# Up projection as seven block products, and the MLP in two phases with its inner tiles in DRAM

## The chip, the core and the metric

The kernel runs on one core of a Trainium2 chip. The metric is the device time of one execution in microseconds; the lower the better. Five engines work on it with queues of their own: TensorE (PE: matmuls; PEld: the loads of their stationary operand), VectorE (DVE), ScalarE (ACT), GpSimd (POOL), and SyncE (SP), which here only issues DMAs. A few DMAs are issued by ScalarE and GpSimd.

## The reference

One encoder layer on x of 1024 tokens x 1024 channels, in float32. Token mixing (a Fourier branch and a dilated window attention, merged by gates, then an output projection) is followed by a normalisation; then comes the part that is changed:

```
h  = layer_norm(ALPHA * x + mix)                       # 1024 x 1024
u  = square(relu(h @ w_up + b_up))                     # 1024 x 4096
ff = u @ w_down + b_down                               # 1024 x 1024
out = layer_norm(ALPHA * h + ff)
```

## The kernel before

**Numbers.** Each float32 operand of a matmul is split into a high part (a cast to fp32r, `nc.scalar.copy`) and a remainder (a subtraction), and one product is three matmuls into the same PSUM bank: high x high, high x remainder, remainder x high (`mm3`, lines 75 to 77). `split` (lines 63, 64) makes the two parts, on ScalarE and VectorE.

**Buffers.** All big tiles come from rings with a fixed count of equal slots: `U` (31 slots of 128 x 1024 floats), `wr` (3, raw weights as they arrive), `w` (10, split weights), `S` (8 of half that size, `half`), `PT` (6 of half size, `tmp`). PSUM has 8 banks under four tags: mm 3, s 2, pt 2, o 1. A new tile waits until a slot of its ring has been given back by everything that read it.

**Order.** The program is written as one stream. A planner (the framework's scheduler) places each instruction on its engine's queue: it simulates the engines with costs of its own, and among the instructions that are ready in that simulation and have a slot it takes the one written first. The queues run in the order so fixed; waits on semaphores hold what the plan had wrong. `with tc.issue_after(ins)` keeps the DMAs of a block behind `ins` in their queue. SP's DMAs are in such an order too, so a DMA that waits for a slot holds those behind it.

**The layer up to the MLP** (lines 80 to 699) isn't changed but for its last loop. That loop (from line 666) makes the output projection for two halves `hf` of the tokens, each in two halves `c` of the channels and four tiles `t` of 128 tokens. When both channel halves of a token tile are there, VectorE, ScalarE and GpSimd normalise it (lines 687 to 697): `h` is the normalised tile and `ac` is ALPHA * h + ALPHA * b1 + b_down, the start of the accumulator `acc`. `transposed` (line 651) then turns `h` on TensorE, four 128 x 128 transposes into one bank, and splits the result out of PSUM into `h1h` and `h1l`, channels on the partitions. The last tiles of a half are turned later (`late`), between other matmuls.

**The MLP before** takes the 4096 inner channels as 32 tiles `f` of 128. The up projection of a tile and a token half `c` is `up_piece` (line 800): 8 k-tiles x 3 matmuls of 128 x 512 into one bank, ReLU with bias on ScalarE, the square on VectorE. The down projection of 14 pairs of tiles uses a scheme with seven block products in place of eight: with inner tiles as A (A11, A12, A21, A22: two tiles by two token halves) and down weights as B (two tiles by two channel halves), `hidden_blocks` and `down_blocks` form sums of blocks (S1 to S4, T1 to T4) and split them; `down_steps` multiplies A11 B11, A12 B21, S2 T2, S3 T3, A22 T4, S1 T1, S4 B22. Several products are added up in the same banks as they go, and after each product VectorE adds the bank into `acc` (line 824). The loop over pairs runs the up pieces of the next pair between the products of this one. The last four tiles (28 to 31) are done plainly by `up` and `down`, and `finish` normalises and stores each token tile. `acc` (8 tiles of U) stays in SBUF all the time.

## Time and profile before

| | |
|---|---|
| median of 3 runs | 1681.54 us (1681.03 to 1685.92) |
| the profiled execution | 1682.96 us, of which 1680.9 us is its span from the first to the last instruction |
| TensorE's granted clock, mean | 0.992 |
| output projection ends | about 972.5 us into the span |
| busy in the span | PE 1632.9, PEld 1328.6, DVE 866.3, ACT 552.9, POOL 377.1 us |

In the rows of the profile "L64" is a line of the kernel (helpers have one line for all their callers), "w<-wr,w" says which tile is written from which, "x119" is the count, and what follows the last bar is the engine's idle time just before these instructions, with what ended it. Matmuls overlap one another, so the mean of one matmul (some 400 ns) is not what one costs.

### The profile page before, as it was taken

The page shows a single profiled execution, that of the slowest core. Times are in us where ns is not written, and L with a number is a line of the kernel's source. Part 1 is how long each engine was busy: PE and PEld are TensorE (multiplying, and loading weights), DVE is VectorE, ACT ScalarE, POOL GpSimd, SP SyncE. Part 2 cuts the span into 40 slices and gives each one's busy share as a digit, 9 for nine tenths or more (in the row PEclk, how much of TensorE's full clock was granted, in tenths as well). Part 3 has the DMA queues.
Part 4 walks back from the last instruction along what each step waited for, and adds up shares of the span by engine and source line. Part 5 has one row for each costly group of instructions (what it writes and reads, how often), then busy time and mean ns, then how long its engine had stood idle before and what let it go on. Part 6 is the DMA issues. An engine that isn't in the chain of part 4 may idle for free.

```text
span 1680.9 us, 20802 instructions
## 1 busy us (share of the span) xinstructions
PE 1632.9 (97%) x7948; PEld 1328.6 (79%) x7948; DVE 866.3 (52%) x1663; ACT 552.9 (33%) x1160; POOL 377.1 (22%) x359
## 2 busy tenths in 40 slices
PE   8999999999999989999999988999999999999997
PEld 6779777897777778888887766777777777777785
DVE  4240322212342566654257767666666666666658
ACT  4150433313453542322124243333333333333322
POOL 0000000000000120000003246444444444444204
PEclk9999999999999999999999999999999999999998
DMA  7210211111111243552133201111111111111212
GB/s 219 79 49 20 81 60 45 45 51 54 46 57 68 90 142 115 160 160 82 38 132 115 92 26 41 49 51 50 50 50 50 51 50 51 51 50 51 79 40 94
DMA packets 47069, 121.19 MB, mean 72 GB/s; under 512 B 8648, under 2 KB 12168, under 8 KB 46970
## 3 DMA queue, kind: packets, MB, share of 16 engines
q1 hardware_dynamic: 43866, 113.28, 20.7%
q0 software_dynamic: 1824, 6.39, 1.0%
q8 instruction: 62, 1.02, 0.3%
q10 hardware_dynamic: 1280, 0.20, 0.1%
q14 instruction: 37, 0.30, 0.1%
HBM read 108.97 MB, written 10.88 MB: 71 GB/s over the span
## 4 chain that ended last, share of the span: by engine, by line
PE 86%; DVE 5%; ACT 3%; issue 3%; POOL 2%; DMA 1%; DVEq 0%; SPq 0%; POOLq 0%; ACTq 0%
PE pmm L75 20%; PE pmm L76 19%; PE pmm L77 19%; PE ps L75 4%; PE ps L77 4%; PE ps L76 4%; PE ppt L75 3%; PE ppt L77 3%; PE ppt L76 3%; PE po L291 2%; PE ps L237 2%; ACT prob L248 2%; PE ppt L262 2%; DVE z L871 1%; ACT o L303 1%
## 5 line engine op out<-in xcount | busy, mean ns | idle before, releaser
L64 DVE TENSOR_TENSOR w<-wr,w 128x1024 fp32r<-128x1024 f32 x119 | 148.1, 1247 | 299.1 <-ACT w L63 291.5
L75 PE MATMUL pmm<-xh,w 128*128 128x512 f32 x640 | 253.2, 396 | 0.5 <-ACT gate L344 0.5
L77 PE MATMUL pmm<-xh,w 128*128 128x512 f32 x640 | 253.5, 396 | 0.0
L76 PE MATMUL pmm<-xl,w 128*128 128x512 f32 x640 | 252.7, 395 | 0.0
L63 ACT CAST w<-wr 128x1024 fp32r<-128x1024 f32 x119 | 125.0, 1051 | 322.2 <-PE pmm L76 251.0
L75 PE MATMUL pmm<-h1h,w 128*128 128x512 f32 x512 | 202.7, 397 | 0.0
L76 PE MATMUL pmm<-h1l,w 128*128 128x512 f32 x512 | 202.4, 395 | 0.0
L77 PE MATMUL pmm<-h1h,w 128*128 128x512 f32 x512 | 201.9, 394 | 0.0
L76 PEld LDWEIGHTS pmm<-xl,w 128*128 128x128 f32 x640 | 120.2, 188 | 29.2 <-issue 1.2
L75 PEld LDWEIGHTS pmm<-xh,w 128*128 128x128 f32 x640 | 120.3, 188 | 28.7 <-issue 1.5
L77 PEld LDWEIGHTS pmm<-xh,w 128*128 128x128 f32 x640 | 120.2, 188 | 28.0 <-issue 0.7
L824 DVE TENSOR_TENSOR z<-z,ps 128x512 f32<-128x512 f32 x168 | 114.1, 680 | 33.6 <-PE ps L77 33.6
L755 POOL TENSOR_TENSOR part<-q,part 128x512 fp32r<-128x512 f32 x84 | 114.4, 1388 | 38.0 <-ACT part L745 38.0
L75 PEld LDWEIGHTS pmm<-h1h,w 128*128 128x128 f32 x512 | 96.6, 189 | 23.5 <-ACT h1h L63 0.3
L77 PEld LDWEIGHTS pmm<-h1h,w 128*128 128x128 f32 x512 | 96.5, 188 | 23.0
L824 DVE TENSOR_TENSOR z<-z,ppt 128x512 f32<-128x512 f32 x168 | 114.2, 679 | 0.0
L76 PEld LDWEIGHTS pmm<-h1l,w 128*128 128x128 f32 x512 | 96.7, 189 | 21.9
L806 DVE TENSOR_TENSOR q<-PT 128x512 f32<-128x512 f32 x56 | 46.3, 827 | 129.9 <-ACT PT L805 129.9
L277 POOL MEMSET pt<- 64x128 f32 x80 | 16.0, 200 | 378.2 <-PE po L291 350.4
L248 ACT ACTIVATE prob<-prob,st 128x192 f32<-128x192 f32 (+2 forms) x192 | 83.9, 438 | 30.9 <-DVE st L245 30.5
L745 ACT CAST part<-wr 128x512 fp32r<-128x512 f32 x84 | 50.6, 620 | 116.2 <-PE pmm L76 61.6
L697 POOL TENSOR_TENSOR z<-z,b_down 128x1024 f32<-128x1024 f32 x8 | 20.9, 2616 | 300.3 <-ACT z L691 300.3
(352 smaller groups left out, 3161.9 us busy)
## 6 DMA issues: line engine op xcount, KB each, us to landing
wr<-in_wup_dram SPq DMA_DIRECT2D x32, 512.0 KB
wr<-in_wdn_dram SPq DMA_DIRECT2D x32, 512.0 KB
wr<-in_wqk_dram SPq DMA_DIRECT2D x24, 512.0 KB
wr<-in_wout_dram SPq DMA_DIRECT2D x16, 512.0 KB
od<-o POOLq DMA_DIRECT2D x12, 512.0 KB, 3.0
PT<-od SPq DMA_DIRECT2D x24, 256.0 KB
PT<-ad SPq DMA_DIRECT2D x48, 128.0 KB
wr<-in_wv_dram SPq DMA_DIRECT2D x11, 512.0 KB
```

The costliest lines, as they stand in the source:

```text
L63: nc.scalar.copy(h, src)
L64: nc.vector.tensor_tensor(l, src, h.bitcast(F32), op=ALU.subtract)
L75: nc.tensor.matmul(o, lh, rh, start=first, stop=False, skip_group_check=on)
L76: nc.tensor.matmul(o, lh, rl, start=False, stop=False, skip_group_check=on)
L77: nc.tensor.matmul(o, ll, rh, start=False, stop=last, skip_group_check=on)
L237: nc.tensor.matmul(pp[hh][:, step * i:step * i + n], q[r, 128 * b:128 * b + 128], k[r, k0:k0 + n], start=True, stop=True)
L248: nc.scalar.activation(e, e, AF.Exp, bias=m, scale=-1.0, accum_out=st[:, 1, hh, b:b + 1])
L262: nc.tensor.transpose(p[0:p1 - p0, 128 * slot:128 * slot + 128], probs[u][hh][:, i, c0:c0 + p1 - p0], ident)
L745: nc.scalar.copy(t[:, 0], src)
L755: pool(t[:, 1], src, t[:, 0].bitcast(F32), op=ALU.subtract)
L806: nc.vector.tensor_tensor(q, r, r, op=ALU.mult)
L824: nc.vector.tensor_tensor(z, z, p, op=ALU.add)
```

## The change

**Up projection.** Inner tiles are now taken in 16 pairs, and each pair (256 inner channels x 1024 tokens, over 1024 input channels) is computed by seven block products in place of eight: A is the pair's weights (two tiles by two halves of the input channels), B the turned tokens (two channel halves by two token halves). One product is 4 k-tiles x 3 matmuls into one bank. The token blocks B11, B21, T2, T3, T4, T1, B22 are made once, in two parts of 256 columns (`e`), by `plain_block` and `token_blocks`: 28 tiles of U. `transposed` now only copies the turned rows out of PSUM. The weight blocks are made per pair by `weight_tiles` (loads) and `weight_blocks` (sums on VectorE, splits on ScalarE and VectorE). A pair runs in three steps: `step0` (A11 B11, A12 B21), `step1` (S2 T2, S1 T1, S3 T3), `step2` (S4 B22, A22 T4). Bank x goes through A11 B11, S2 T2, S3 T3, A22 T4 and is copied by ScalarE after each of the first three (`keep`); bank z holds S1 T1, then S4 B22 on top; `joined` adds a copy and a bank on VectorE. The `step0` of the first four pairs (START) needs only the first token half and is run ahead of the rest.

**DRAM.** The accumulator's start goes to DRAM (`accd`) and comes back at the start of the down phase. GpSimd forms the sums of the inner blocks, and the seven blocks of each of the 14 pairs are saved to DRAM unsplit (`qd`): A11, A22 and A12 by DMAs that ScalarE issues, S1 to S4 by GpSimd. The last two pairs' inner tiles are saved plainly (`qp`).

**Down projection.** It starts when all inner tiles are done, in groups of four pairs (the last has two). For each of the seven products the A blocks of the group's pairs are read back two at a time, cast on ScalarE, the remainder on GpSimd; the B blocks are made from the raw down weights, which are loaded two pairs to a tile in pieces of 2 KB. The product of all pairs of the group is added up in the bank before VectorE adds it to `acc`. The last four inner tiles are read back and done plainly, with `finish` as before.

```diff
+    accd = dram.tile([8, 128, 1024], F32, name="accd")
     late = []
+    raw = {}
+    TB = {n: ([], []) for n in ("B11", "B21", "T2", "T3", "T4", "T1", "B22")}
     def transposed(hf, t, h):
         tc_ = slice(128 * t, 128 * t + 128)
...
             for i in range(2):
                 dp = 2 * q + i
                 if t == 0:
...
+                    raw[hf, dp] = U([128, 2, 512], name="h1t")
+                (nc.vector.tensor_copy if i else nc.scalar.copy)(
+                    raw[hf, dp][:, :, tc_], p[:, 256 * i:256 * i + 256].rearrange("p (d n) -> p d n", d=2))
+        if hf == 0 and t == 3:
+            plain_block("B11", 0)
+        if hf == 1 and t == 3:
+            for i in range(2):
+                token_blocks(i, 1)
+    def plain_block(name, d0):
+        for dp in range(d0, d0 + 2):
+            h_, l_ = U([128, 2, 512], F32R, "tb"), U([128, 2, 512], F32R, "tb")
+            split(raw[0, dp], h_, l_)
+            for v, x in zip(TB[name], (h_, l_)):
+                v.append(x)
+    def token_blocks(i, e):
+        cs = slice(256 * e, 256 * e + 256)
+        b11, b21, b12, b22 = (raw[f, d][:, :, cs] for f, d in ((0, i), (0, 2 + i), (1, i), (1, 2 + i)))
+        sub = nc.vector.tensor_tensor
+        def put(name, src, eng=nc.vector):
+            if e == 0:
+                for v in TB[name]:
+                    v.append(U([128, 2, 512], F32R, "tb"))
+            h_, l_ = (v[i][:, :, cs] for v in TB[name])
+            nc.scalar.copy(h_, src)
+            eng.tensor_tensor(l_, src, h_.bitcast(F32), op=ALU.subtract)
+        t3 = tmp([128, 2, 256], name="t3")
+        nc.gpsimd.tensor_tensor(t3, b22, b12, op=ALU.subtract)
+        sub(b12, b12, b11, op=ALU.subtract)
+        sub(b11, b22, b12, op=ALU.subtract)
+        put("T2", b11)
+        put("T3", t3, nc.gpsimd)
+        sub(b21, b21, b11, op=ALU.subtract)
+        put("T4", b21)
+        put("T1", b12)
+        put("B22", b22, nc.gpsimd)
+    def weight_tiles(pair, both=True):
+        r = []
+        for i in range(2 if both else 1):
+            r.append((U if i and START < pair < 15 else wr)([128, 1024], name="wup"))
+            last = nc.sync.dma_start(r[i], a["wup"][2 * pair + i].rearrange("p k c -> p (k c)"))
+        WR[pair] = r, last.ins
+    def weight_blocks(pair, which):
+        (wa, *wb), _ = WR.pop(pair)
+        out = WB[pair]
+        def put(name, src):
+            t = out[name] = wh([128, 2, 512], F32R, "wb")
+            split(src, t[:, 0], t[:, 1])
+        sum_ = nc.vector.tensor_tensor
+        a11, a12 = wa[:, :512], wa[:, 512:]
+        if which != 1:
+            put("A11", a11)
+            put("A12", a12)
+        if which == 0:
+            return
+        a21, a22 = wb[0][:, :512], wb[0][:, 512:]
+        s3 = tmp([128, 512], name="s3")
+        sum_(s3, a11, a21, op=ALU.subtract)
+        sum_(a21, a21, a22, op=ALU.add)
+        sum_(a11, a21, a11, op=ALU.subtract)
+        put("S2", a11)
+        put("S1", a21)
+        put("S3", s3)
+        sum_(a12, a12, a11, op=ALU.subtract)
+        put("S4", a12)
+        put("A22", a22)
+    START = 4
+    WB = [{} for _ in range(16)]
+    WR = {}
...
                     nc.gpsimd.tensor_tensor(ac, ac, bdn, op=ALU.add)
-                    acc.append(ac)
+                    nc.sync.dma_start(accd[4 * hf + t], ac)
                     late.append((hf, t, h))
...
+    def block_steps(pair):
+        w = WB[pair]
+        ba, bb = bup[:, 2 * pair:2 * pair + 1], bup[:, 2 * pair + 1:2 * pair + 2]
+        bank, part = {}, {}
+        def product(x, y, b, tag=None):
+            first = tag is not None
+            if first:
+                bank[b] = ps(tag)
+            for k in range(4):
+                ks = slice(128 * k, 128 * k + 128)
+                h_, l_ = (v[k // 2][:, k % 2] for v in TB[y])
+                mm3(bank[b], w[x][:, 0, ks], w[x][:, 1, ks], h_, l_, first and k == 0, k == 3, True)
+        def keep(name):
+            part[name] = tmp([128, 512], name="part")
+            nc.scalar.copy(part[name], bank["x"])
+        def done(name, src, bias):
+            r, q = tmp([128, 512]), half([128, 512], name="q")
+            nc.scalar.activation(r, src, AF.Relu, bias=bias)
+            nc.vector.tensor_tensor(q, r, r, op=ALU.mult)
+            return q
+        def joined(name, b):
+            t = part[name]
+            nc.vector.tensor_tensor(t, t, bank[b], op=ALU.add)
+            return t
+        pool = nc.gpsimd.tensor_tensor
+        q = {}
+        strassen = pair < PAIRS
+        def save(name, t):
+            if strassen:
+                (nc.gpsimd if name[0] == "S" else nc.scalar).dma_start(qd[pair, NAMES.index(name)], t)
+        def plain(i, c, t):
+            if not strassen:
+                nc.scalar.dma_start(qp[2 * (pair - PAIRS) + i, :, 512 * c:512 * c + 512], t)
+        def step0():
+            product("A11", "B11", "x", "o" if pair == 3 else "mm")
+            keep("r1")
+            product("A12", "B21", "y", "pt")
+            q[11] = done("A11", joined("r1", "y"), ba)
+            save("A11", q[11])
+            plain(0, 0, q[11])
+        def step1():
+            product("S2", "T2", "x")
+            keep("r2")
+            product("S1", "T1", "z", "s")
+            product("S3", "T3", "x")
+            keep("r3")
+            q[22] = done("A22", joined("r3", "z"), bb)
+            save("A22", q[22])
+            plain(1, 1, q[22])
+        def step2():
+            product("S4", "B22", "z")
+            q[21] = done("A21", joined("r2", "z"), ba)
+            plain(0, 1, q[21])
+            if strassen:
+                s3 = half([128, 512], name="q")
+                pool(s3, q[11], q[21], op=ALU.subtract)
+                save("S3", s3)
+                pool(q[21], q[21], q[22], op=ALU.add)
+                save("S1", q[21])
+                pool(q[11], q[21], q[11], op=ALU.subtract)
+                save("S2", q[11])
+            product("A22", "T4", "x")
+            q[12] = done("A12", bank["x"], bb)
+            save("A12", q[12])
+            plain(1, 0, q[12])
+            if strassen:
+                s4 = half([128, 512], name="q")
+                pool(s4, q[12], q[11], op=ALU.subtract)
+                save("S4", s4)
+        return [step0, step1, step2]
+    NAMES = ("A11", "A12", "S2", "S3", "A22", "S1", "S4")
+    PAIRS = 14
+    qd = dram.tile([PAIRS, 7, 128, 512], F32, name="qd")
+    qp = dram.tile([32 - 2 * PAIRS, 128, 1024], F32, name="qp")
+    plain_block("B21", 2)
+    for x in range(START):
+        weight_tiles(x, False)
+        weight_blocks(x, 0)
+    steps = [block_steps(x) for x in range(16)]
+    for x in range(START):
+        steps[x][0]()
+        if x == 0:
+            while late:
+                if late[0][1] == 3:
+                    for i in range(2):
+                        token_blocks(i, 0)
                 transposed(*late.pop(0))
...
+    for x in range(2):
+        weight_tiles(x)
+    weight_blocks(0, 1)
+    for x in range(16):
+        if x < 13:
+            weight_tiles(x + 2)
+        if x < 15:
+            weight_blocks(x + 1, 2 if START <= x + 1 < 15 else 1)
+        if x == 13:
+            weight_tiles(15, False)
+            weight_blocks(15, 0)
+            weight_tiles(15)
+            last = WR[15][1]
+        steps[x][1]()
+        for nxt in {13: (14, 15), 14: ()}.get(x, (x + 1,)):
+            if START <= nxt < 16:
+                steps[nxt][0]()
+        steps[x][2]()
+        WB[x].clear()
+    def b_raw(pair):
+        r = {}
+        for i in range(2):
+            for c in range(2):
+                t = r[i, c] = U([128, 2, 512])
+                nc.sync.dma_start(t, a["wdn"][2 * pair + i:2 * pair + i + 3:2, :, 512 * c:512 * c + 512]
+                                  .rearrange("b p n -> p b n"))
+        return r
+    def b_raws(p0, n):
+        return [b_raw(p0 + d) for d in range(0, n, 2)]
+    def rest_raws():
+        r = []
+        for f in range(2 * PAIRS, 32):
+            r.append(U([128, 1024], name="wdn"))
+            nc.sync.dma_start(r[-1], a["wdn"][f])
+        return r
+    load = [None]
+    with tc.issue_after(last):
+        r0 = b_raws(0, 4)
+    acc = []
+    with tc.issue_after(last):
         for t in range(8):
...
+            acc.append(U([128, 1024], name="acc"))
+            nc.sync.dma_start(acc[t], accd[t])
+    def a_block(name, pair):
+        r = wr([128, 2, 512])
+        load[0] = nc.sync.dma_start(r, qd[pair:pair + 2, NAMES.index(name)].rearrange("b p n -> p b n")).ins
+        h_, l_ = U([128, 2, 512], F32R), U([128, 2, 512], F32R)
+        nc.scalar.copy(h_, r)
+        nc.gpsimd.tensor_tensor(l_, r, h_.bitcast(F32), op=ALU.subtract)
+        return h_, l_
+    def b_split(src):
+        h_, l_ = wh([128, 2, 512], F32R), wh([128, 2, 512], F32R)
+        split(src, h_, l_)
+        return h_, l_
+    ORDER = (("A11", "B11"), ("A12", "B21"), ("S2", "T2"), ("S3", "T3"), ("A22", "T4"), ("S1", "T1"), ("S4", "B22"))
+    def b_block(name, r):
+        b11, b12, b21, b22 = r[0, 0], r[0, 1], r[1, 0], r[1, 1]
+        sub = nc.vector.tensor_tensor
+        if name == "B11":
+            return b_split(b11)
+        if name == "B21":
+            return b_split(b21)
+        if name == "T2":
+            t3 = r["t3"] = U([128, 2, 512])
+            nc.gpsimd.tensor_tensor(t3, b22, b12, op=ALU.subtract)
+            sub(b11, t3, b11, op=ALU.add)
+            return b_split(b11)
+        if name == "T3":
+            return b_split(r["t3"])
+        if name == "T4":
+            sub(b21, b21, b11, op=ALU.subtract)
+            return b_split(b21)
+        if name == "T1":
+            sub(b12, b22, b11, op=ALU.subtract)
+            return b_split(b12)
+        return b_split(b22)
+    def add_up(p0, n, r, then):
+        def blocks(i):
+            x, y = ORDER[i]
+            return [a_block(x, p0 + d) for d in range(0, n, 2)], [b_block(y, v) for v in r]
         bank = {}
...
+        chain, side = ("s", "s", "pt", "pt"), ("mm", "mm", "mm", "o")
+        def product(tags, new, lo, c, A, B):
             for t in range(4):
...
+                if new:
+                    bank[tags, t] = ps(tags[t])
+                p = bank[tags, t]
+                ts = slice(128 * t, 128 * t + 128)
+                for d in range(n // 2):
+                    for e in range(2):
+                        mm3(p, A[d][0][:, e, ts], A[d][1][:, e, ts], B[d][0][:, e], B[d][1][:, e],
+                            new and d == e == 0, d == n // 2 - 1 and e == 1, True)
                 z = acc[t + lo][:, 512 * c:512 * c + 512]
                 nc.vector.tensor_tensor(z, z, p, op=ALU.add)
...
+        todo = ((chain, True, 0, 0), (side, True, 0, 0), (chain, False, 0, 1), (chain, False, 4, 1),
+                (chain, False, 4, 0), (side, True, 4, 1), (side, False, 0, 1))
+        nxt = blocks(0)
+        for i, how in enumerate(todo):
+            cur = nxt
+            if i < 6:
+                nxt = blocks(i + 1)
+            if i == 4:
+                with tc.issue_after(load[0]):
+                    out = then()
+            product(*how, *cur)
+        return out
+    GROUPS = ((0, 4), (4, 4), (8, 4), (12, 2))
+    for i, (p0, n) in enumerate(GROUPS):
+        r0 = add_up(p0, n, r0, (lambda: b_raws(*GROUPS[i + 1])) if i < 3 else rest_raws)
     g2, b2 = row("ln2_g"), row("ln2_b")
...
+    rest = []
+    for f in range(2 * PAIRS, 32):
+        x, y = wr([128, 1024]), r0[f - 2 * PAIRS]
+        nc.sync.dma_start(x, qp[f - 2 * PAIRS])
+        v = [U([128, 1024], F32R) for _ in range(2)] + [wh([128, 1024], F32R) for _ in range(2)]
+        nc.scalar.copy(v[0], x)
+        nc.gpsimd.tensor_tensor(v[1], x, v[0].bitcast(F32), op=ALU.subtract)
+        split(y, v[2], v[3])
+        rest.append(v)
+    for t in range(8):
+        for c in range(2):
+            s = slice(512 * c, 512 * c + 512)
+            ts = slice(128 * t, 128 * t + 128)
+            p = ps(("s", "pt")[c])
+            for i, (xh_, xl_, yh_, yl_) in enumerate(rest):
+                mm3(p, xh_[:, ts], xl_[:, ts], yh_[:, s], yl_[:, s], i == 0, i == len(rest) - 1)
+            nc.vector.tensor_tensor(acc[t][:, s], acc[t][:, s], p, op=ALU.add)
+        finish(t)
```

More of the change, by code (lines that the diff above doesn't have):

```diff
@@ L697, in tile_hybrid_layer @@
                     nc.gpsimd.tensor_tensor(ac, ac, bdn, op=ALU.add)
-                    acc.append(ac)
+                    nc.sync.dma_start(accd[4 * hf + t], ac)
                     late.append((hf, t, h))
-    hid = {}
-    def up(fs):
-        w = {f: wup[f] if f in wup else weights(a["wup"][f], [128, 8, 128]) for f in fs}
-        for f in fs:
-            hid[f] = U([128, 1024], F32R, "hid"), []
-        for c in range(2):
-            while c and late:
-                transposed(*late.pop(0))
-            for f in fs:
-                p = ps("mm")
-                for k in range(8):
-                    mm3(p, w[f][0][:, k], w[f][1][:, k], h1h[c, k // 2][:, k % 2], h1l[c, k // 2][:, k % 2],
-                        k == 0, k == 7)
-                r, q = tmp([128, 512]), tmp([128, 512])
-                nc.scalar.activation(r, p, AF.Relu, bias=bup[:, f:f + 1])
-                nc.vector.tensor_tensor(q, r, r, op=ALU.mult)
-                l = half([128, 512], F32R, "hidl")
-                split(q, hid[f][0][:, 512 * c:512 * c + 512], l)
-                hid[f][1].append(l)
@@ L722, in down @@
-    def down(fs, after):
-        w = [weights(a["wdn"][f], [128, 1024]) for f in fs]
-        for t in range(8):
-            for c in range(2):
-                s = slice(512 * c, 512 * c + 512)
-                p = ps(("s", "pt")[c])
-                for i, f in enumerate(fs):
-                    hh, ls = hid[f]
-                    mm3(p, hh[:, 128 * t:128 * t + 128], ls[t // 4][:, 128 * (t % 4):128 * (t % 4) + 128],
-                        w[i][0][:, s], w[i][1][:, s], i == 0, i == len(fs) - 1)
-                nc.vector.tensor_tensor(acc[t][:, s], acc[t][:, s], p, op=ALU.add)
-            after(t)
@@ L741, in tile_hybrid_layer @@
-    PAIRS = 14
-    def parts(src, make):
-        t = make([128, 2, 512], F32R, "part")
-        nc.scalar.copy(t[:, 0], src)
-        return t
-    def hidden_blocks(out, q, j):
-        pool = nc.gpsimd.tensor_tensor
-        def put(name, src):
-            t = out[name] = parts(src, U)
-            pool(t[:, 1], src, t[:, 0].bitcast(F32), op=ALU.subtract)
-        if j == 0:
-            put("A11", q[0])
-        elif j == 1:
-            s3 = tmp([128, 512], name="cmb")
-            pool(s3, q[0], q[1], op=ALU.subtract)
-            put("S3", s3)
-        elif j == 2:
-            put("A12", q[2])
-        else:
-            pool(q[1], q[1], q[3], op=ALU.add)
-            pool(q[0], q[1], q[0], op=ALU.subtract)
-            put("S2", q[0])
-            put("A22", q[3])
-            pool(q[2], q[2], q[0], op=ALU.subtract)
-            put("S1", q[1])
-            put("S4", q[2])
@@ L800, in up_piece @@
-    def up_piece(w, f, c):
-        p = ps("mm")
-        for k in range(8):
-            mm3(p, w[0][:, k], w[1][:, k], h1h[c, k // 2][:, k % 2], h1l[c, k // 2][:, k % 2], k == 0, k == 7)
-        r, q = tmp([128, 512]), half([128, 512], name="q")
-        nc.scalar.activation(r, p, AF.Relu, bias=bup[:, f:f + 1])
-        nc.vector.tensor_tensor(q, r, r, op=ALU.mult)
-        return q
-    def up_weights(f):
-        return wup[f] if f in wup else weights(a["wup"][f], [128, 8, 128])
-    def down_steps(A, B):
+    def block_steps(pair):
[68 more added lines that the diff above has]
+        return [step0, step1, step2]
@@ L823, in product @@
                 z = acc[t + lo][:, 512 * c:512 * c + 512]
                 nc.vector.tensor_tensor(z, z, p, op=ALU.add)
-        def alone(x, y, c, lo):
-            held = dict(bank)
-            product(x, y, True, c, lo, ("mm",))
-            bank.update(held)
-        return [lambda: (product("A11", "B11", True, 0, 0), alone("A12", "B21", 0, 0)),
-                lambda: (product("S2", "T2", False, 1, 0), product("S3", "T3", False, 1, 4)),
-                lambda: (product("A22", "T4", False, 0, 4), product("S1", "T1", True, 1, 4)),
-                lambda: product("S4", "B22", False, 1, 0)]
@@ L877, in finish @@
             nc.sync.dma_start(out[128 * t:128 * t + 128, s], z[:, s])
-    down(range(2 * PAIRS, 32), finish)
+    rest = []
[16 more added lines that the diff above has]
+        finish(t)
 def onehot():
```

67 lines of the change are left out of this document (removed).

## The prediction

> **What bounds the kernel now.** I read the page first, then the busy time by stretches of the span, then the chain that ended last, and only then the groups of instructions. The page says that TensorE is busy for nearly the whole span:
>
> ```profile
> span 1680.9 us, 20802 instructions
> PE 1632.9 (97%) x7948; PEld 1328.6 (79%) x7948; DVE 866.3 (52%) x1663; ACT 552.9 (33%) x1160; POOL 377.1 (22%) x359
> ```
>
> Ends of matmuls are modelled, so the share alone proves little. I cut the span at the points where the chain of waits leaves TensorE and comes back to it: the end of the output projection (972.5 us), the steady state of the MLP (1020.1), and the point from which VectorE's last normalisations set the pace (1641.6). Columns: stretch, length, then busy time and (count) of PE, PEld, DVE, ACT, POOL, then clock, DMA share, GB/s.
>
> ```profile
> 972.50:1020.10 47.60, 37.29 (x163) 29.36 (x162) 31.39 (x47) 18.86 (x37) 26.18 (x15) 0.96 0.10 31
> 1020.10:1641.60 621.50, 621.02 (x2647) 496.71 (x2648) 391.82 (x608) 183.23 (x287) 262.97 (x201) 1.00 0.15 52
> 1641.60:1681.00 39.40, 27.80 (x120) 22.17 (x118) 34.85 (x72) 9.55 (x18) 18.01 (x12) 0.89 0.25 94
> ```
>
> The middle stretch has 0.5 us without a matmul in 621.5 us, with VectorE at 63% and all the others lower. The MLP is bound by the number of its matmuls, apart from its two ends. The chain that ended last shows the price of one: the same matmul comes back once per pair of hidden tiles,
>
> ```profile
> 1064.75 0.44 PE pmm L75
> ...
> 1106.89 0.43 PE pmm L75
> ...
> 1149.02 0.44 PE pmm L75
> ```
>
> and between two of these lie 96 matmuls of the up projection (4 pieces x 8 x 3) and 84 of the down projection (7 products x 4 x 3). (1149.02 - 1064.75) / 360 = 0.2341 us each.
>
> **The change, part by part.** *Matmuls removed.* Up: 32 x 2 x 8 x 3 = 1536 before; 16 pairs x 7 products x 4 k-tiles x 3 = 1344 after. Down: 14 x 84 + 192 = 1368 before and after, and the 64 transposes stay. So 192 fewer, all from a stretch in which nothing else sets the pace: 192 x 0.2341 = **-44.9 us**. This count is fixed by the code. What follows is what can eat it.
>
> *What the other engines get in steady state.* Prices, from the groups of instructions (busy, mean ns of one):
>
> ```profile
> L64 DVE TENSOR_TENSOR mgl<-mg,mgh 128x512 fp32r<-128x512 f32 x16 | 10.5, 686 | 5.5 <-PE pmm L76 3.5 <-ACT mgh L63 2.1
> L591 DVE TENSOR_TENSOR mg<-mg,gate 128x512 f32<-128x512 f32 x16 | 11.0, 690 | 0.4
> L824 DVE TENSOR_TENSOR z<-z,ps 128x512 f32<-128x512 f32 x168 | 114.1, 680 | 33.6 <-PE ps L77 33.6
> L806 DVE TENSOR_TENSOR q<-PT 128x512 f32<-128x512 f32 x56 | 46.3, 827 | 129.9 <-ACT PT L805 129.9
> L64 DVE TENSOR_TENSOR w<-wr,w 128x1024 fp32r<-128x1024 f32 x119 | 148.1, 1247 | 299.1 <-ACT w L63 291.5 <-PE pmm L76 7.5
> L63 ACT CAST w<-wr 128x1024 fp32r<-128x1024 f32 x119 | 125.0, 1051 | 322.2 <-PE pmm L76 251.0 <-PE ppt L77 24.8 <-DMA wr<-in_wqk_dram 9.2
> L745 ACT CAST part<-wr 128x512 fp32r<-128x512 f32 x84 | 50.6, 620 | 116.2 <-PE pmm L76 61.6 <-PE pmm L77 32.1 <-PE ppt L77 18.2
> L805 ACT ACTIVATE PT<-pmm,bup 128x512 f32<-128x512 f32 x56 | 38.4, 685 | 112.7 <-PE pmm L77 112.7
> L203 ACT COPY qk<-pmm 128x512 f32<-128x512 f32 x24 | 14.0, 584 | 45.5 <-PE pmm L77 45.5
> L755 POOL TENSOR_TENSOR part<-q,part 128x512 fp32r<-128x512 f32 x84 | 114.4, 1388 | 38.0 <-ACT part L745 38.0
> L479 POOL TENSOR_TENSOR sin<-wr,sin 128x1024 fp32r<-128x1024 f32 x2 | 4.9, 2448 | 4.0 <-ACT sin L478 4.0
> L64 DVE TENSOR_TENSOR h1l<-ps,h1h 128x256 fp32r<-128x256 f32 x32 | 13.0, 418 | 3.7 <-ACT h1h L63 3.2
> ```
>
> Saving and loading, from the answers on single tiles, and the GB/s row in 40 slices of the span:
>
> ```profile
> L322 ACTq DMA_DIRECT2D sd<-ss x16: 270/317/566, 100.1 to 249.2; - x16
> L313 POOL DMA_DIRECT2D od<-o x12: 531/531/691, 100.8 to 567.1; - x12
> L806 DVE TENSOR_TENSOR q<-PT x56: 682/692/2173, 985.7 to 1559.7; 128x512 f32<-128x512 f32 x56
> od<-o POOLq DMA_DIRECT2D x12, 512.0 KB, 3.0
> GB/s 219 79 49 20 81 60 45 45 51 54 46 57 68 90 142 115 160 160 82 38 132 115 92 26 41 49 51 50 50 50 50 51 50 51 51 50 51 79 40 94
> ```
>
> A pair of the up phase is 84 x 0.2341 = 19.7 us of TensorE. VectorE: 7 splits and 4 sums at 0.69, 4 squares at 0.83, 3 joins with a bank at 0.68 = 12.9 us. ScalarE: 7 casts at 0.62, 3 copies out of PSUM at 0.58, 4 ReLUs at 0.69, 3 saves at 0.32 = 9.8. GpSimd: 4 sums at 1.39, 4 saves at 0.53 = 7.7. A group of four pairs in the down phase is 336 x 0.2341 = 78.7 us of TensorE against 14 splits and 6 sums at 1.25 and 28 adds at 0.68 = 44 on VectorE, 28 casts at 1.05 = 29 on ScalarE, 14 + 2 passes at 2.45 = 39 on GpSimd. The adds into the accumulator fall from 392 to 112, which pays for VectorE's new work; none of it was on the path, so it earns nothing. DMA: a pair moves 1.05 MB in and 1.84 MB out (147 GB/s), a group 11.5 MB (146 GB/s), three times the MLP's 50 of now, under the 160 to 219 of other slices. All stays hidden as long as no single wait outlasts its cover. Between S2's product and S3's, into the same bank, ScalarE's copy of the bank has one product of cover (2.8 us); between S3 and S4 lie two products of the next pair, except for pairs 0 to 2 and 14, 15, where the next pair's S2 can step in. Bounds for stalls here: none, and 18 us (12 pairs x 1.5, see the second rival); I take 2, since the loop of now, which is as full (VectorE 63%, 12.9 / 19.7 = 65% after), loses 0.5 us in all.
>
> *The start.* The transposes of the normalised rows in this stretch, from the answer on their line and one row of the timeline:
>
> ```profile
> L657 PE MATMUL ps<-ident,h x24: 270/273/476, 972.6 to 994.8; 128*128 128x128 f32 x24
> 994.02 1.06 PE L657 MATMUL ps<-ident,h 128*128 128x128 f32 x8 [2.42 <-DVE h1l L64]
> ```
>
> Before, from 972.5 to 1020.1, TensorE had 163 - 24 transposes = 139 matmuls (32.5 us) and 24 x 0.13 = 3.2 us of transposes: 11.9 us lost. After, it has 96 matmuls on the first token half (step0 of pairs 0 to 3), the 24 transposes, and S2 of pair 0: 25.7 + 2.8 = 28.5 us, to 1001.0. Then it needs T1 of the tokens, which needs the last transposed rows.
>
> ```profile
> 970.00:980.00 10.00, 7.11 (x29) 5.43 (x28) 9.69 (x17) 6.32 (x13) 3.76 (x3) 0.83 0.34 104
> 980.00:990.00 10.00, 10.00 (x50) 8.16 (x48) 7.86 (x13) 4.03 (x8) 7.27 (x4) 1.00 0.01 3
> ```
> ```profile
> 988.11 1.37 DVE L696 SCALAR_TENSOR_TENSOR h<-h,lnq,ln_b 128x1024 f32<-128x1024 f32 x1 [1.48 <-ACT z L691]
> ```
> ```profile
> 994.68 1.67 ACT L63 CAST h1h<-ps 128x256 fp32r<-128x256 f32 x4 [1.33 <-PE ps L657]
> ```
>
> Busy time in two slices of it, the last of the last rows, and four copies out of the transposes' banks, are shown above. From below: the rows are done at 989.5, plus 1.1 for transposes, 1.7 for copies, 12 VectorE operations at 0.69 = 8.3: T1 at 1000.6, nothing lost, **-11.9**. In between: VectorE's own queue. Of its 17.6 us in 970 to 990 about 8.6 are splits that go (8 h1l, two w, three part, one square), 9.0 of normalisation stay; 6 copies at 0.42, 6 weight splits at 0.69, B21's two at 1.25, four joins and squares (5.5), 24 token operations at 0.69 (16.6), 3 sums and 2 splits of pair 0's weights (3.4) make 43.6 us: T1 at 1016.1, 15.1 lost, **+3**. From above, GpSimd's 12 token operations (3 in each of 4 calls) are held against VectorE's. At 1010 to 1020, where GpSimd never rests, both slow down:
>
> ```profile
> 1012.03 1.76 POOL L794 TENSOR_TENSOR wr<-wr,wr 128x512 f32<-128x512 f32 x1
> 1013.75 1.72 POOL L755 TENSOR_TENSOR part<-q,part 128x512 fp32r<-128x512 f32 x1
> 1015.43 1.72 POOL L767 TENSOR_TENSOR q<-q,q 128x512 f32<-128x512 f32 x1
> ```
> ```profile
> 1012.56 1.78 DVE L784 TENSOR_TENSOR part<-cmb,part 128x512 fp32r<-128x512 f32 x1
> 1014.47 4.91 DVE L784 TENSOR_TENSOR part<-wr,part 128x512 fp32r<-128x512 f32 x3
> ```
>
> One operation of each takes about 1.7 us, a VectorE operation 1.0 more than its 0.69: 12 x 1.0 more, T1 at 1028, 27 lost, **+15**. I take +3: the lower bound forgets a queue that was 88% full for these 20 us already.
>
> The Trainium skill (SBUF — State Buffer, section "Who interferes with whom") says that a VectorE instruction with two SBUF inputs contends with a GpSimd instruction that reads SBUF, and that the one issued first blocks the other for its whole length. The trace agrees nearly: 1.72 us for the couple, where 0.69 and 1.3 added give 2.0. By the page's full sum an up pair would need 15 x 0.69 + 7.7 = 18 of its 19.7 us, so the steady part would still be hidden, and the start and the end would be the first rival below.
>
> *The boundary of the phases.* The tokens' 28 U tiles leave 3 of 31. B11's and B21's 8 come free after step0 of pair 15, 144 matmuls (33.7 us) before the up phase ends, enough for the 8 loads of down weights; T2's, T1's and T3's go next, to the accumulator's loads and to the first A11, which needs 1.05 + 2.45 us of cast and remainder while S4 and A22 still run (5.6 us). Nothing lost is the lower bound; the upper is a load (3.0), a cast and two GpSimd passes in a row, 3.0 + 1.05 + 4.9 = 9. I take **+2**. Behind a wait of SP here stand only loads that are needed later.
>
> *The end.* The last group has two pairs, 168 matmuls, 39.3 us, and beside it the last four tiles are read back and split: GpSimd 8 + 4 passes at 2.45 = 29.4, VectorE 7 + 3 + 4 operations at 1.25 = 17.5 plus adds that read PSUM. Hidden if they overlap, 47 - 39 = 8 late if they exclude each other. I take **+2**. The normalisations behind it are unchanged.
>
> Sum: -44.9 + 3 + 2 + 2 + 2 = -35.9 on the profiled execution's 1682.96 us: 1647. The median shown, 1681.54, is 1.4 lower, so **1646** for the median.
>
> **Rivals.** (1) *VectorE and GpSimd exclude each other where TensorE has no cover*, at the start (+15) and before the last four tiles (+8): -44.9 + 15 + 8 + 2 + 2 = 1665. For it: the 1.7 us couples. Against: only 12 GpSimd operations meet the start. (2) *A wait per pair in ScalarE's order.* The ring w has 10 tiles and a pair takes 7, so the next pair's last cast waits until S1's product gives its tile back; if the copy of the bank is queued behind it, S3 waits for 0.62 + 0.58 and hand-overs, 1.5 us, in 12 pairs: 18, so 1663. Against: the planner orders by readiness, and the same kind of ring holds now without loss. (3) *Slower than before*, the same queue carried on: ScalarE also issues saves, and a save waits for VectorE's square. Cast behind S1 (2.81 + 0.62), a square held by GpSimd (2.17, the longest in the row), the issue (0.32) and the copy (0.58) are 6.5 us against 2.8 of cover: 3.7 us in 14 pairs, 52, so 1682.96 - 44.9 + 52 + 7 = 1697. It decides from 2.5 us of standstill in every pair on. Against: the longest square is one of 56, the median is 0.69. (4) *The start gains*: T1 is there in time, -11.9, with 6 for the rest: 1632. (5) *(1) and (2) together*: -1.5, no change.
>
> **How the numbers follow.** Forecast (1638 to 1656) 0.48; (1) 0.17; (2) 0.11; (3) 0.08; (4) 0.12; (5) 0.04. Less than 0.3% (5 us) can't be told from no change here. Faster: 0.48 + 0.17 + 0.11 + 0.12 = 0.88; same 0.04; slower 0.08. The range takes in (1), (2) and most of (4): 1630 to 1674.
>
> **What would show it.** TensorE's count is 7756. In the up phase a pair's period is 19.7 us (rival 2: 21 or more, with gaps between S1 and S3 released by ScalarE; rival 3: 23). Between the output projection's last matmul and S1 of pair 0 some 15 us are lost, ended by VectorE (rival 4: under 5; rival 1: 25, with VectorE's token splits at 1.7 us). A group of the down phase takes 78.7 us. At the boundary there is one gap of a few us, ended by GpSimd or a load. The forecast is wrong if gaps stand inside the groups, ended by a DMA: then the traffic of 146 GB/s, which I take as hidden, is what I misjudged.

## The result, and the profile after

The changed kernel takes 1740.9 us (median, 1739.7 to 1748.7), the kernel before beside it 1681.6: a ratio of 1.0358 (95% interval 1.0328 to 1.0387), slower. The forecast was 1646. The execution that was profiled took 1748.72 us, 65.8 more than that of before. The page after:

```profile
span 1746.9 us, 20677 instructions
PE 1625.9 (93%) x7756; PEld 1319.0 (76%) x7756; DVE 971.6 (56%) x1551; ACT 607.0 (35%) x1194; POOL 398.5 (23%) x333
```

The 192 matmuls are gone (7948 to 7756), but TensorE's busy time fell by 7.0 us only, and the time in which it stands rose from 48 to 121 us. Busy time by stretches of the changed kernel (columns as in the prediction: stretch, length, busy and count of PE, PEld, DVE, ACT, POOL, clock, DMA share, GB/s). They are the start, pairs 0 to 3, pairs 4 to 13, pairs 14 and 15, the boundary with the first group of the down phase, and the rest of that phase:

```profile
972.50:1040.00 67.50, 42.74 (x164) 33.34 (x165) 57.30 (x82) 32.57 (x56) 32.73 (x18) 0.78 0.27 92
1040.00:1110.00 70.00, 63.36 (x240) 48.36 (x239) 52.06 (x56) 25.24 (x43) 23.47 (x24) 0.89 0.36 134
1110.00:1350.00 240.00, 203.86 (x796) 160.89 (x794) 159.04 (x172) 79.81 (x133) 77.62 (x79) 0.91 0.30 112
1350.00:1400.00 50.00, 45.12 (x178) 35.47 (x179) 28.04 (x34) 19.59 (x30) 8.54 (x10) 0.93 0.76 263
1400.00:1450.00 50.00, 42.14 (x176) 33.12 (x175) 39.66 (x29) 19.92 (x22) 39.23 (x14) 0.97 0.50 149
1450.00:1690.00 240.00, 240.00 (x1027) 193.88 (x1027) 181.52 (x159) 82.50 (x83) 132.10 (x46) 0.99 0.44 141
```

The down phase is what was forecast: 240.00 of 240 us busy, with 141 GB/s beside it. The up phase is not: in 240 us VectorE is busy for 66% and the DMA engines for 30%, nothing is full, and yet TensorE stands for 36 us and its clock is 0.91. I took the start of every matmul in the trace and added up what lies beyond 0.234 us between two starts: as idle time where the distance is over 0.5 us, as half clock where it is 0.33 to 0.5.

| stretch | idle | half clock | both | expected in the prediction |
|---|---|---|---|---|
| start, to 1040 (before, to 1020.1: 11.2 + 1.0) | 26.2 | 5.9 | +19.9 against before | +3 |
| pairs 0 to 3 | 9.1 | 5.3 | 14.4 | |
| pairs 4 to 13 | 42.6 | 15.4 | 58.1 | |
| pairs 14 and 15 | 4.2 | 1.2 | 5.4 | all pairs together +2 |
| boundary, first group | 8.7 | 0.8 | 9.5 | +2 |
| 1450 to 1690 | 0.0 | 1.7 | 1.7 | +2 (end) |

With the -44.9 of the matmuls that is +64.1; the kernel before loses 6.0 behind 1020.1 by the same measure, so +58.1 are left. The MLP of the two profiled executions, from the start of the output projection's last matmul to the end of the span, takes 708.7 us before and 767.8 after: 59.1 more, as the medians have it (59.3). The other 6.9 of the 65.8 lie ahead of the MLP, behind 5019 matmuls in both kernels. This is where that last matmul starts, first before, then after:

```profile
972.14 0.40 PE L77 MATMUL pmm<-w,mgl 128*128 128x512 f32 x1
979.07 0.40 PE L77 MATMUL pmm<-w,mgl 128*128 128x512 f32 x1
```

In the twelve traces of this case it starts anywhere from 966.5 to 979.1, so these 6.9 us are no more than what this part varies by. Seven tenths of the loss in the MLP lie in the pairs. TensorE's waits (what it waited for: us in total, times, longest):

```profile
PE pmm L75 <- ACT part L795: 40.0, 13, 5.9
PE ps L658 <- POOL h L765: 13.9, 4, 7.3
PE ppt L75 <- DVE part L805: 13.1, 1, 13.1
PE pmm L75 <- ACT wb L63: 6.1, 3, 4.0
PE ps L75 <- DVE acc L987: 5.7, 1, 5.7
```

The first row is the copy of bank x behind S2's product (`keep("r2")`, line 795): S3 goes into the same bank. One such pause in the timeline (start, length, engine, instruction; in brackets the idle time ahead of it and what ended it):

```profile
1191.61 1.67 POOL L844 TENSOR_TENSOR q<-q,q 128x512 f32<-128x512 f32 x1 [16.91 <-DVE q L800]
...
1192.91 0.91 DVE L800 TENSOR_TENSOR q<-PT 128x512 f32<-128x512 f32 x1 [0.80 <-issue]
...
1193.57 0.56 POOL L814 DMA_DIRECT2D qd<-q  x1 [0.30 <-POOL q L844]
...
1193.74 2.27 DVE L728 TENSOR_TENSOR wup<-wup 128x512 f32<-128x512 f32 x1
...
1194.15 1.30 POOL L846 TENSOR_TENSOR q<-q,q 128x512 f32<-128x512 f32 x1
...
1196.05 2.14 DVE L729 TENSOR_TENSOR wup<-wup,wup 128x512 f32<-128x512 f32 x1
...
1196.33 1.30 POOL L848 TENSOR_TENSOR q<-q,q 128x512 f32<-128x512 f32 x1
...
1198.23 1.14 ACT L63 CAST wb<-wup 128x512 fp32r<-128x512 f32 x2 [5.40 <-DVE wup L729]
1198.23 2.12 DVE L733 TENSOR_TENSOR wup<-wup 128x512 f32<-128x512 f32 x1
...
1199.27 0.61 ACT L63 CAST wb<-s 128x512 fp32r<-128x512 f32 x1
...
1200.44 0.62 ACT L63 CAST wb<-wup 128x512 fp32r<-128x512 f32 x1 [0.56 <-DVE wup L733]
1200.97 0.58 ACT L795 COPY part<-pmm 128x512 f32<-128x512 f32 x1
...
1201.60 0.80 PE L75 MATMUL pmm<-tb,wb 128*128 128x512 f32 x1 [3.75 <-ACT part L795]
...
1202.19 0.63 PE L76 MATMUL pmm<-tb,wb 128*128 128x512 f32 x1
```

Read from the end: TensorE waits for ScalarE's copy. The copy's source, S2's product, was done at about 1194.8, 6 us earlier; but in ScalarE's queue the copy stands behind four casts of the *next* pair's weight sums (S2', S1', S3', S4'), which TensorE needs only a period later. These wait for VectorE's sums, and the sums take 2.1 to 2.3 us in place of 0.69, because GpSimd forms the inner sums (lines 844 to 856) in the same microseconds. After the pause the matmuls come 0.43 us apart. From 1110 to 1360 there are eight pauses of 3.9 us (4.15 from start to start, as the expectations below have it), one of 6.1 and one of 2.0; a period is 25 us where 19.7 were forecast.

### The profile page after: what moved, and what is told of

The parts are those of the page before. It is cut to its first block, busy times and chain, and to the rows that moved or that the text cites. A ratio compares the mean times of both kernels' runs of the same rounds, so it can differ in the third digit from the quotient of the medians.

```text
span 1746.9 us, 20677 instructions
## 1 busy us (share of the span) xinstructions
PE 1625.9 (93%) x7756; PEld 1319.0 (76%) x7756; DVE 971.6 (56%) x1551; ACT 607.0 (35%) x1194; POOL 398.5 (23%) x333
## 5 line engine op out<-in xcount | busy, mean ns | idle before, releaser
L64 DVE TENSOR_TENSOR w<-wr,w 128x1024 fp32r<-128x1024 f32 x83 | 103.5, 1249 | 293.4 <-ACT w L63 293.4
L63 ACT CAST w<-wr 128x1024 fp32r<-128x1024 f32 x83 | 87.1, 1051 | 234.7 <-PE pmm L76 190.7
L933 POOL TENSOR_TENSOR U<-wr,U 128x1024 fp32r<-128x1024 f32 x49 | 143.3, 2944 | 110.3 <-ACT U L932 48.9
L75 PE MATMUL pmm<-tb,wb 128*128 128x512 f32 x240 | 107.4, 448 | 46.1 <-ACT part L795 40.0
L64 DVE TENSOR_TENSOR w<-U,w 128x1024 fp32r<-128x1024 f32 x49 | 103.3, 2110 | 21.9 <-ACT w L63 18.9
L77 PE MATMUL pmm<-tb,wb 128*128 128x512 f32 x240 | 103.3, 431 | 2.8 <-DVE wb L64 2.8
L76 PE MATMUL pmm<-tb,wb 128*128 128x512 f32 x240 | 103.7, 432 | 0.0
L75 PEld LDWEIGHTS pmm<-tb,wb 128*128 128x128 f32 x240 | 50.9, 212 | 64.6 <-ACT part L795 45.7
L63 ACT CAST w<-U 128x1024 fp32r<-128x1024 f32 x49 | 51.3, 1048 | 126.0 <-PE ppt L76 56.0
L768 POOL TENSOR_TENSOR z<-z,b_down 128x1024 f32<-128x1024 f32 x8 | 19.5, 2440 | 309.3 <-ACT z L762 284.0
L63 ACT CAST wb<-wup 128x512 fp32r<-128x512 f32 x96 | 56.6, 618 | 90.2 <-DVE wup L729 75.0
L245 DVE CUSTOM_DVE_ANT_0 prob<-ps,bias 128x192 f32<-128x192 f32 (+2 forms) x192 | 55.8, 347 | 44.6 <-PE ps L237 37.6
L844 POOL TENSOR_TENSOR q<-q,q 128x512 f32<-128x512 f32 x14 | 23.3, 1665 | 226.7 <-DVE q L800 226.7
```

The lines of the kernel that those rows point to most:

```text
L63: nc.scalar.copy(h, src)
L64: nc.vector.tensor_tensor(l, src, h.bitcast(F32), op=ALU.subtract)
L75: nc.tensor.matmul(o, lh, rh, start=first, stop=False, skip_group_check=on)
L76: nc.tensor.matmul(o, lh, rl, start=False, stop=False, skip_group_check=on)
L77: nc.tensor.matmul(o, ll, rh, start=False, stop=last, skip_group_check=on)
L245: nc.vector.tensor_tensor_reduce(out=e, in0=pp[hh][:, step * i:step * i + n], in1=bias[:, hh, bs], scale=-1.0, scalar=3e38, op0=ALU.add, o ...
```

## The experiments

**Theory A:** GpSimd's inner sums hold VectorE's weight sums, and ScalarE's queue carries that delay to a copy that TensorE waits for. **Rivals:** VectorE has simply too much to do (B); the traffic to and from DRAM (C); for the start, couples (D) against the mere length of VectorE's queue (E). A has two links, so the first three runs cut one, the other, and both. "Before" in the same comparisons was 1682.2 to 1684.6 us.

**The queue's order alone.** `weight_blocks` makes the sums where it did and gives back the five casts, which are written behind the pair's step1 (each with its remainder, so VectorE's order moves a little too):

```diff
-            weight_blocks(x + 1, 2 if START <= x + 1 < 15 else 1)
+            casts = weight_blocks(x + 1, 2 if START <= x + 1 < 15 else 1)
...
         steps[x][1]()
+        if x < 15:
+            with tc.issue_after(mark["r2"]):       # behind the copy, on ScalarE
+                casts()
```

> Only ScalarE's order in the up phase is changed: the copy of S2's bank (keep r2) stands ahead of the casts of the next pair's weight sums; VectorE's sums and GpSimd's inner sums stay where they are, so their couples at 2.2 us stay. Theory A (GpSimd slows VectorE's weight sums, and ScalarE's queue carries the delay to the copy that S3 waits for): the 4.15 us gap per pair goes, and with it the half clock behind it; the up phase loses some 58 us less, at most 5 come back at the join of r3 behind the remainders: 1741 - 53 = 1688, period 20 us. Rival B (VectorE has too much to do, whatever the order): the gap moves to S4, which waits for the join, period 23 or more, 1720 to 1741. Rival C (the DRAM traffic of the up phase): no change, 1741.

Measured 1684.35 us, ratio to before 1.0004 (0.9988 to 1.0019). The couples are all still there, the pauses are not. The row of line 728 among the instructions on this tile (times, shortest/median/longest in ns, from when to when), and the stretch of the steady pairs, both of this run:

```profile
L728 DVE TENSOR_TENSOR wup<-wup x16: 691/2268/2276, 1027.0 to 1313.9; 128x512 f32<-128x512 f32 x16
1110.00:1350.00 240.00, 233.31 (x983) 184.27 (x983) 194.68 (x204) 101.36 (x165) 95.94 (x92) 0.99 0.48 173
```

VectorE is busier (81%), the traffic greater (173 GB/s), and TensorE loses some 0.6 us a pair from 1120 to 1300, where a pair takes 20.1 us. That is A's number, and B and C fall: a fuller VectorE and more traffic per microsecond go with less loss.

**The couples alone.** The inner sums on VectorE, ScalarE's order held:

```diff
-        pool = nc.gpsimd.tensor_tensor
+        pool = nc.vector.tensor_tensor
...
+            with tc.issue_after(mark[pair + 1]):   # behind the cast of S4'
+                nc.scalar.copy(part["r2"], bank["x"])
```

> GpSimd's four inner sums per pair are made on VectorE instead; ScalarE's order is held as it was, the copy of S2's bank behind the four casts. Theory A: VectorE's sums fall from 2.2 to 0.69 us; from the square of A12 to the end of the copy it is 5 sums (3.5), a cast and the copy (1.2), 4.7 us where it was 8.2; S3 could start 3.9 us after the square, so a gap of about 0.9 us per pair is left: 58 - 14 x 0.9 = 45 less, 1696. A rival that has the queue's order alone as its cause (contention without effect): the gap stays near 4, 1741. Rival B (too much work on VectorE, which gets 2.8 us more per pair): gaps of over 4, 1741 to 1770.

Measured 1674.35 us, 0.9937 (0.9915 to 0.9960). Line 728's counterpart and the same stretch of this run:

```profile
L730 DVE TENSOR_TENSOR wup<-wup x16: 682/684/692, 1023.7 to 1305.9; 128x512 f32<-128x512 f32 x16
1110.00:1350.00 240.00, 238.93 (x1028) 191.75 (x1027) 168.70 (x246) 101.20 (x166) 45.87 (x49) 1.00 0.51 179
```

The sums are at 0.68 us and the copy, still behind the casts, is in time; the 0.9 us a pair that I had left over for it don't show (a steady pair takes 19.6). So the order alone doesn't lose the time either: it takes both links.

**Both.** The first line of that diff alone; with it the planner itself puts the copy ahead of the casts.

> GpSimd's four inner sums per pair on VectorE, and ScalarE's order left to the planner, which now has the copy of S2's bank ahead of the next pair's casts: both suspected causes are gone. Theory A: no gap above 0.5 us in a pair, period 19.7 us, 1741 - 56 = 1685; the start loses its 23 us still. Rival B (VectorE is full: 15.7 of 19.7 us per pair): period over 21, above 1705. Rival C (traffic): 1741.

Measured 1664.59 us, 0.9883 (0.9862 to 0.9904), faster than before. From 1040 on:

```profile
1040.00:1110.00 70.00, 70.00 (x303) 56.30 (x302) 53.86 (x87) 30.41 (x53) 8.67 (x16) 1.00 0.48 176
1110.00:1350.00 240.00, 238.39 (x1026) 192.26 (x1025) 171.54 (x241) 103.08 (x161) 50.74 (x51) 1.00 0.49 175
```

Every pair takes 19.5 us. It is 20 us better than expected, since I had kept the loss of pairs 0 to 3, 14 and 15 (14.4 + 5.4) as it was, and it went with the same edit.

For the rest, this table goes by the count of matmuls, from the eight transposes ahead of the output projection's last 24 matmuls: the first 204 (32 transposes, those 24, and 148 of the up phase; some 44 us of work), then the mean of 13 times 84 (a pair), and, from 72 matmuls further on, 336 that reach over the boundary into the first group (78 where nothing stalls). The last column is the MLP of the profiled execution, from the projection's last matmul to the end of the span; before it was 708.7. What varies ahead of the MLP from execution to execution is not in these four columns, but it is in the median.

| run | median | ratio to before (95%) | first 204 | a pair | first group | MLP |
|---|---|---|---|---|---|---|
| the change | 1740.9 | 1.036 (1.033 to 1.039) | 77.0 | 25.1 | 89.4 | 767.8 |
| queue's order alone | 1684.4 | 1.000 (0.999 to 1.002) | 75.8 | 20.9 | 87.6 | 709.1 |
| couples alone | 1674.4 | 0.994 (0.992 to 0.996) | 77.2 | 20.4 | 86.8 | 698.2 |
| both | 1664.6 | 0.988 (0.986 to 0.990) | 75.4 | 19.5 | 88.6 | 687.0 |
| tokens on VectorE, nothing else | 1738.4 | 1.031 (1.029 to 1.033) | 71.9 | 25.4 | 87.7 | 764.3 |
| both, new order of the start | 1659.3 | 0.986 (0.982 to 0.989) | 71.7 | 19.5 | 88.4 | 683.1 |
| new order, tokens on VectorE | 1654.8 | 0.981 (0.978 to 0.984) | 69.2 | 19.5 | 88.6 | 681.0 |
| new order, copy first | 1656.0 | 0.984 (0.982 to 0.986) | 66.9 | 19.7 | 87.9 | 680.5 |
| new order, copy first, tokens on VectorE | 1650.8 | 0.981 (0.979 to 0.983) | 62.9 | 19.7 | 88.6 | 677.2 |
| the last, and one more row tile on VectorE | 1650.8 | 0.981 (0.979 to 0.983) | 61.9 | 19.7 | 88.8 | 676.5 |
| new order, copy first, tokens and T3 of the down weights on VectorE | 1649.6 | 0.978 (0.976 to 0.981) | 63.2 | 19.7 | 84.8 | 673.5 |

**The start: couples.** In the changed kernel, `token_blocks` with no GpSimd operation (three of its instructions moved to VectorE).

> The start alone: the 12 token operations of GpSimd (T3 and the remainders of T3 and B22) are made by VectorE, 36 in place of 24 there. Theory D (each engine holds the other, 1.7 us a couple): 24 at about 1.7 us become 36 at 0.69, 41 to 25 us, and the gaps of TensorE between 972 and 1040 us fall by 10 to 16: 1741 - 13 = 1728. Rival E (only the length of VectorE's queue ahead of the joins counts, which is 12 longer): no gain, 1741 to 1750. The up phase behind it stays as it was.

Measured 1738.44 us. TensorE's waits in this run:

```profile
PE ppt L75 <- DVE part L805: 7.5, 1, 7.5
PE pmm L75 <- ACT wb L63: 8.7, 3, 6.6
```

The pause for the joins (line 805) fell from 13.1 to 7.5, with 12 more operations in VectorE's queue, so the couples have a part in it (D); but the next one, for pair 0's weight casts, grew from 4.0 to 6.6. The first 204 matmuls gained 5.1 us and the total 2.5, not 13. Something else in that queue is behind it.

**The start: the order on VectorE.** On top of "both", the queue in the order in which TensorE needs it (shortened; `token_blocks_2` takes T4 and B22 over from `token_blocks`):

```diff
         put("T2", b11)
+        put("T1", b12)
         put("T3", t3, nc.gpsimd)
-        sub(b21, b21, b11, op=ALU.subtract)
-        put("T4", b21)
-        put("T1", b12)
-        put("B22", b22, nc.gpsimd)
...
+        if x == 1:                               # behind step0 of pairs 0 and 1
+            for e in range(2):
+                for i in range(2):
+                    token_blocks(i, e)
+            for y in range(2):
+                weight_tiles(y)
+            weight_blocks(0, 1)
...
+    for e in range(2):                           # behind step0 of pairs 2 and 3
+        for i in range(2):
+            token_blocks_2(i, e)                 # T4 and B22
```

> On top of the inner sums on VectorE (1664.6), only the order of the start: VectorE gets the joins of pairs 0 and 1, then the token operations of T2, T1 and T3, then pair 0's weight sums, then the joins of pairs 2 and 3, and T4 and B22 last. Theory D (S2 of pair 0 comes late because VectorE's queue holds the joins, T4 and B22 ahead of its weight sums): from the join of pair 1 (996) 16 token operations with couples (18 us), four sums and one remainder (4.2): S2 at 1018 instead of 1028.6, so 10 less, 1655. Rival F (something outside VectorE's order sets the start: the last transposed rows, the loads of the weights): gain under 3, 1662 to 1667.

> The same order, and besides no GpSimd work on tokens (T3 and the remainders of T3 and B22 on VectorE) and all copies out of the transposes' banks on ScalarE: no couples in the start. Theory D with couples: 24 token operations at 0.61 (14.6) and 4.2 behind the join of pair 1, S2 at 1015, the copies 2 more: 13 to 15 less than 1664.6, 1650. If the couples cost as much as the operations they replace, it is level with the run before it. Rival F: no gain, 1662 to 1667.

Measured 1659.32 and 1654.83 us. In the first, S2 of pair 0 starts 38.9 us behind the output projection's last matmul in place of 54.9, 15.9 us earlier; of that, 3.7 are left at the end of the first 204 matmuls. TensorE's waits in its start say where the rest went:

```profile
PE ps L658 <- POOL h L769: 7.3, 1, 7.3
PE pmm L75 <- ACT part L799: 5.6, 1, 5.6
PE pmm L75 <- ACT wb L63: 2.9, 1, 2.9
PE ps L75 <- DVE part L809: 2.6, 1, 2.6
```

The second row is the old acquaintance: the copy of S2's bank, now behind the casts of T4 and B22, whose sources VectorE hadn't made. I had written them there myself. So the next run moves them behind step1:

```diff
         steps[x][1]()
+        if x == 0:
+            for e in range(2):
+                for i in range(2):
+                    token_blocks_2(i, e)
```

> The run with the new order of the start (1659.3), and only T4's and B22's token operations are written behind pair 0's step1, so that ScalarE's copy of S2's bank stands ahead of all but one of their casts. Theory (the same cause as in the up phase: a copy that TensorE waits for stands behind casts whose source is late): the gap of 6.0 us in front of S3 of pair 0 falls below 1, and with the half clock behind it 5 to 7 us go: 1653. Rival G (VectorE, which has no pause from 1000 to 1037 there, sets the pace, so the gap only moves to S4): 1657 to 1661.

> The same step on the run without GpSimd work on tokens (1654.8), whose gap in front of S3 is 3.5 us: by the theory 3 to 4 us less, 1651; by rival G no change, 1653 to 1656.

Measured 1655.95 and 1650.84 us, 3.4 and 4.0 less. The waits in the start of the first:

```profile
PE ps L658 <- POOL h L769: 7.8, 2, 7.3
PE pmm L75 <- ACT wb L63: 7.1, 2, 3.8
PE pmm L75 <- ACT part L799: 1.7, 2, 1.0
```

The copy's wait is gone (5.6 to 1.0 at most). The intervals of these runs overlap with those above them, so for single steps of 3 to 5 us the traces speak (the MLP is 2.6 and 3.8 us shorter) and the times only agree; over all four steps, 1664.6 to 1650.8, the intervals are apart. The rival of a full VectorE has its share: the 84 matmuls after it take 21.9 us where they took 19.5, so part of the gain is given back there.

**A pause that costs little.** One of TensorE's longest waits in the start is for GpSimd's `h` (line 765 of the change). One more token tile's last step goes to VectorE:

```diff
-                    if t < 3:
+                    if t < 3 - hf:
```

> On top of that run, the last step (+ b1) of one more token tile's normalisation (tile 2 of the second half) is made by VectorE in place of ScalarE and GpSimd: TensorE's queue holds that tile's transposes ahead of step0's products, and waits 6 to 7 us for GpSimd's pass there. If this wait costs the end its full length: 5 us less, 1646. If the 6 us are only idle time ahead of a stretch that VectorE sets: no gain, 1650 to 1653.

Measured 1650.83 us: no gain. The pause shrank from 6.1 to 4.0 us (from start to start), the first 204 matmuls by 1.0 and the MLP by 0.7. Behind it TensorE still waits 7.3 us for the weight casts of pair 0, which VectorE's queue sets.

**The boundary.** `t3` in `b_block` is made on VectorE.

> On the run at 1650.8 with all of these steps, one more for the boundary of the phases: T3 of the down weights (GpSimd, 2.4 us a sum, which stand behind six remainders of 2.7) is made on VectorE. There the first group waits 5.6 us for VectorE's add into the accumulator, behind T2's sums, which wait 4.1 us for GpSimd and then take 3.4 us each. Theory (the same cause again, a queue that carries GpSimd's delay): the gap of 6.0 us in the first group goes, with 2 us of half clock behind it, 6 to 8 less: 1643 to 1645. Rival (what is late there are the blocks read back from DRAM): the gap stays, ended by ScalarE, GpSimd or a load, 1649 to 1652.

Measured 1649.56 us. TensorE's wait in the first group, first of the run that this one is built on (1650.8), then of this one:

```profile
PE ps L75 <- DVE acc L996: 5.6, 1, 5.6
PE ps L75 <- DVE acc L996: 2.9, 1, 2.9
```

The group went from 88.6 to 84.8 and the MLP from 677.2 to 673.5: half of what was expected, and the time can't tell 1.3 us. So GpSimd's sum is part of this pause; what makes up the other half is open.

## Why the prediction was wrong

- *Matmuls removed, -44.9:* right. 7756, as counted, and with the pauses gone the pairs take 19.5 us (19.7 forecast) and the groups of the down phase 77.9 (78.7).
- *"What the other engines get in steady state", +2, bounds 0 and 18:* the step that failed, by 76 us (14.4 + 58.1 + 5.4 = 77.9 lost in the pairs). Its engine sums were nearly right: VectorE had 12.9 us of work a pair, and 159.04 us in 240 at a period of 25 are 16.6, the difference being about what three couples add. The inference from them failed. That the loop of now "is as full" says nothing on order: in the changed loop a copy that TensorE waits for stands behind casts whose source two other engines hold up, 3.9 us in most pairs. The upper bound was wrong as well, since it took its price (1.5 us) from a wait for a ring slot.
- *The Trainium skill's rule* (SBUF — State Buffer, "Who interferes with whom"): the durations nearly agree, 0.69 and 1.30 add to 1.99 and the sums took 2.12 to 2.27. What I drew from it, that 18 of 19.7 us "would still be hidden", holds for throughput only: with every couple in place and ScalarE's order mended, a steady pair takes 20.1 us. In the change the 4.5 us more latency in one chain passed through two queues in order, and that the sum doesn't show.
- *Rival 2* had the place (ScalarE's order, a gap between S1 and S3 ended by ScalarE, a period over 21) and the wrong source and price. *Rival 3* was the right side, with its point of decision (2.5 us of standstill; it was 3.9 in most pairs), but the late thing was a weight sum, not a square. "The planner orders by readiness" was my argument against rival 2. The plan put the casts ahead, so by its costs the sums must have been ready; whether these costs know of couples is not shown. (*Rivals 1 and 2 together* add up to -1.9, not the -1.5 of the prediction; nothing hangs on it.)
- *The half clock* is in no term of the pairs: 30 us of the table, all stretches together (6 before, by the same measure). A pause of 3.9 us cost a pair 5.5 (25.0 where 19.5 are possible).
- *The start, +3, bounds -11.9 and +15:* +19.9, beyond the upper bound. The step counted VectorE's queue up to T1 and let TensorE go on from there. But S2 of pair 0 needs the weight sums, which stood behind all token operations and three joins (it started 55.9 us behind the projection's last matmul; in the prediction it is done 28.5 us behind it), and the joins, behind the token operations too, kept the banks (13.1 us). The length of the queue was the right thing to look at; its order wasn't looked at. The couples that made my upper bound, and *rival 1*, are a part: without them the start gained 5 us, the order and the copy brought 8.5.
- *The boundary, +2 (0 to 9):* 9.5, the size off; the gap was ended by VectorE's add, behind GpSimd's sums, not by a load. *The end, +2:* nothing was lost there.
- *The traffic,* named as what would make the forecast wrong, was harmless: 175 to 179 GB/s in pairs without a pause.

The last version reaches 1649.6 us, 33 less than before, of the 44.9 that the matmuls give; the start and the first group keep most of the rest.

## What to carry to other kernels

Sums of busy time per engine say whether a loop can be hidden; whether it is hidden is decided by what stands ahead of the one instruction that TensorE waits for, in each queue it passes. Go through the queues for work that is needed much later but written earlier, above all where its source comes from an engine that another one slows down. And price a pause that comes back in every period with the half clock behind it, not by its length alone.

## What the runs showed of the hardware

**The clock.** In the MLP of the kernel before, of the changed one and of its variants, every pause of TensorE between two 128x512 matmuls that lasted 3.03 us or more was followed at once by matmuls 0.43 us apart, 6 to 14 of them. Single pauses of 1.7 and 2.8 us were followed by 0.23; one of 2.0 had it three matmuls later, and several of 1.0 to 1.6 us within a few microseconds had it too. The Trainium skill (TensorE: Matmul & The Clock Gate, "Why this matters for your kernels") asks for no idle gaps over about 3 us; the traces agree, with the edge for a single pause between 2.8 and 3.0.

**The couples.** In the timeline above VectorE's sum of line 728 starts at 1193.74, while GpSimd still issues a DMA (1193.57 to 1194.13) and 0.41 us ahead of GpSimd's next sum (line 846); it ends at 1196.01, 0.56 after that sum. Line 729 starts 0.28 ahead of line 848 and ends 0.56 after it. By the Trainium skill's rule (SBUF — State Buffer, "Who interferes with whom") the one that issues first blocks the other, so VectorE should have gone first. The DMA's issue alone doesn't hold VectorE: in the run with both links cut GpSimd only issues DMAs from 1040 to 1310, and 56 of VectorE's operations with two inputs in SBUF start within such an issue and take 0.68 to 0.69 us, as these do:

```profile
1209.83 0.54 POOL L814 DMA_DIRECT2D qd<-q  x1 [15.35 <-DVE q L844]
1210.05 0.69 DVE L846 TENSOR_TENSOR q<-q,q 128x512 f32<-128x512 f32 x1
```

Why the sum that is recorded as the first loses stays open; the recorded starts may mislead.
